# A hybrid attention encoder on one core: rotary's exchange moved from DMA to ScalarE, attention steps placed later, output casts ordered behind V's copy

## The chip, the cores and the metric

The kernel runs on one NeuronCore of one Trainium2 chip. The engines are named as in the profile: PE is TensorE's matrix multiply, PEld its weight load, DVE is VectorE, ACT is ScalarE, POOL is GpSimd, SP is SyncE, which issues this kernel's DMAs from one queue in order (SPq). Every engine takes its instructions in the order in which they stand in its program. The metric is the time of one execution on the device in microseconds.

## The reference

One encoder layer is applied to two groups of requests, a prompt of 1024 tokens and a sample of 256, each with 16 learned meta tokens in front. Cut to what matters:

```python
def encoder_layer(h, norm_w, w_in, q_norm_a, k_norm_a, q_norm_b, k_norm_b, rpb, w_out, rope_tabs):
    u = rms_norm(h, norm_w) @ w_in
    qa, ka, va, za, qb, kb, vb, zb = jnp.split(u, split_points(), axis=-1)
    qa = apply_axial_rope(rms_norm(qa.reshape(B, N, 8, 128), q_norm_a), rope_tabs)
    ka = apply_axial_rope(rms_norm(ka.reshape(B, N, 2, 128), k_norm_a), rope_tabs)
    ya = global_gqa(qa, ka, va) * jax.nn.silu(za)
    qb = rms_norm(qb.reshape(B, N, 8, 128), q_norm_b)
    kb = rms_norm(kb.reshape(B, N, 8, 128), k_norm_b)
    yb = neighbourhood_attention(qb, kb, vb, rpb) * jax.nn.silu(zb)
    return h + jnp.concatenate([ya, yb], axis=-1) @ w_out

def _rotate(x, cos, sin):
    x1, x2 = jnp.split(x, 2, axis=-1)
    return jnp.concatenate([x1 * c - x2 * s, x1 * s + x2 * c], axis=-1)
```

`h` has 2048 columns, a head has 128. The eight heads of group A (with two shared K/V heads) see all tokens; the eight of group B see a window of the grid and have a bias table `rpb`. Rotary works on each half of a head's 128 channels for itself: the first 32 channels of a half are combined with its last 32. With channels on the partitions, as here, the four blocks of 32 partitions are exchanged pairwise, 0 with 1 and 2 with 3.

## The kernel before, in words

**Arithmetic.** Everything is fp32. A product is made of three matmuls: each operand is cast by ACT to a high part (`split`, L65, L203) and DVE subtracts it from the original for a low part (L66); high x high, high x low and low x high are summed in PSUM (L219 to L221 in the projection, L368 to L370 and L409 to L411 in the attention, L1038 to L1040 in the output projection).

**Projection in strips.** `w_in` is cut into 52 strips of 128 columns: a head's K, Q, V or gate z of group A or B. Tokens form two chunks. Chunk one holds 512 (16 meta tokens, the sample, 240 of the prompt), chunk two the other 784, in blocks of 512 and 272. `strips` runs one strip: four weight chunks of 4 x 128 rows, each loaded by SP (L198), split into wh and wl, and used by 12 matmuls per block. In chunk one the low part is also stored (L210). After the second and the fourth weight chunk, that is twice a strip, it calls `run_due`, which starts what is due at that place: a head's scores, a head's values. Chunk two's attention of group B follows a list of such places too.

**Draining a strip.** `qk_evac` takes the strip's sum out of PSUM: ACT squares it into ms (L252), POOL sums over the partitions (L254, an all-reduce), DVE adds eps (L255), and `rsqrt` takes the inverse root (L72, L74, L75 on ACT, L76 and L77 on DVE). With rotary ACT also copies the sum times the gain to t (L258); four DMAs issued by SP copy t to ts with the blocks of 32 partitions exchanged (L261); DVE multiplies t by cosines (L263, in place) and ts by signed sines (L264), adds them (L265), and multiplies by the inverse root (L268). Then q or k is split. Rotary happens for 2 K and 8 Q strips in each chunk, with one block a strip in chunk one and two in chunk two: 30 drains. A strip of V is multiplied by the token scale into vt (`v_rows`, L280), transposed by PE in pieces of 128 columns into the PSUM tile tp, of which there is one (L287, L531), copied out by ACT (`rows_out`, L533, L538) and stored.

**Attention of chunk one.** After a head's Q strip `later` files the two halves of its attention under two later places: the scores and the softmax up to the sum under the first number of `PARTS`, the values and the output under the second, both counted in calls of `run_due` from there. `PARTS` is 2, 6. In group A two strips (z, q) lie between heads, in group B four. The attention is `attend` for group A and `attend_sample` for group B. An attention takes the maximum over partitions on POOL (L319), subtracts it on DVE (L388), takes exponentials on ACT (L389), sums (L334, L337 on POOL), splits the exponentials to ph and pl, and multiplies with V into po; `put_y` inverts the sum (L344 to L347) and stores the head's output (L355). While chunk one projects group B, `w_sums` also loads pieces of `w_out` and takes differences of them on DVE (L587), which are stored for the output projection.

**Output projection.** It runs in seven products over half matrices. `w_load` (L1012) brings a 128 x 512 piece of `w_out` into the buffers that the projection's x has left, `w_operand` splits it to wm (L65, L66), `y_load` (L976) brings an output tile in two halves, `y_operand` splits these, and `products` multiplies. The first sixteen pieces and the first tile are prepared while the last strips (V and then z of head 7 in group B) are still being projected. The last heads' attention runs beside the first product.

**Order.** The kernel is laid out by a scheduler at compile time, which runs a timing model of its own and orders each engine's instructions by it; `issue_after` and `add_manual_dep` with `NoSync` bind only the order on one engine.

Of the kernel before, what the change touches and what calls it, by code (L numbers as in the profile page):

```python
# [15 lines left out]
AF = mybir.ActivationFunctionType  # L16
ALU = mybir.AluOpType
# [27 lines left out]
WTYPE = (0, 1, 1, 2)  # L45
FILL = 1
LATE = 48
PARTS = 2, 6
WCH = 4
LAG = 6  # L50
TH = (NP + NS) // 2
# [1 line left out]
FB = 512  # L53
FH = DM // 2
QA, KA, VA, ZA, QB_, KB, VB, ZB = 0, 8, 10, 12, 20, 28, 36, 44
AGAIN = {KA, VA, ZA} | {a + h for a in (QB_, KB, VB, ZB) for h in range(4, 8)}


class Kern:
# [3 lines left out]
    def split(self, hi, lo, full):  # L63
        nc = self.nc
        self.hi = nc.scalar.copy(hi, full).ins  # L65
        return nc.vector.tensor_tensor(out=lo, in0=full, in1=hi.bitcast(F32), op=ALU.subtract).ins  # L66

    def rsqrt(self, ms, n):

        nc = self.nc  # L70
        l = self.ev.tile([P, n], F32, tag="ev", name="rs_l")
        nc.scalar.activation(l[:], ms, AF.Ln)  # L72
        r0 = self.ev.tile([P, n], F32, tag="ev", name="rs_r0")
        nc.scalar.activation(r0[:], l[:], AF.Exp, scale=-0.5)  # L74
        nc.scalar.activation(l[:], r0[:], AF.Square, scale=0.5 ** 0.5)  # L75
        nc.vector.tensor_tensor(out=l[:], in0=ms, in1=l[:], op=ALU.mult)  # L76
        nc.vector.scalar_tensor_tensor(out=r0[:], in0=l[:], scalar=1.5, in1=r0[:], op0=ALU.subtract, op1=ALU.mult)  # L77
        return r0
# [105 lines left out]
    def strips(self, jobs, getx):  # L184
# [4 lines left out]
        for c in range(KT // WCH):  # L189
            ws = []  # L190
            behind = self.behind.pop(0) if self.behind else None
            for j, (s, _, _) in enumerate(jobs):
                wp = self.w if j < 2 else self.w1
                with tc.high_priority(offset=self.woff), tc.issue_after(behind) if behind else nullcontext():
# [5 lines left out]
                    wl = wp.tile([P, WCH, P], F32R, tag="wl", name="wl")  # L200
                    if self.second and s not in AGAIN:
                        nc.sync.dma_start(wl[:].bitcast(F32), self.wld[s][:, c * WCH:(c + 1) * WCH, :])
# [5 lines left out]
                ws.append((wh, wl))  # L208
                if not self.second and s not in AGAIN:
                    nc.sync.dma_start(self.wld[s][:, c * WCH:(c + 1) * WCH, :], wl[:].bitcast(F32))  # L210
# [38 lines left out]
    def qk_evac(self, ps, o, n, wc, rope, segs, full=None):  # L249
        nc = self.nc  # L250
        ms = self.ev.tile([P, n], F32, tag="ev", name="ms")
        nc.scalar.activation(ms[:], ps[:, :n], AF.Square, scale=P ** -0.5)  # L252
        m2 = self.ev.tile([P, n], F32, tag="ev", name="m2")
        nc.gpsimd.partition_all_reduce(m2[:], ms[:], P, RED.add)  # L254
        nc.vector.tensor_tensor(out=m2[:], in0=m2[:], in1=self.eb[:, o:o + n], op=ALU.add)  # L255
        if rope is not None:
            t = self.ev.tile([P, n], F32, tag="ev", name="t")
            nc.scalar.activation(t[:], ps[:, :n], AF.Copy, scale=wc)  # L258
            ts = self.ev.tile([P, n], F32, tag="ev", name="ts")
            for i in range(4):  # L260
                nc.sync.dma_start(ts[32 * i:32 * i + 32], t[32 * (i ^ 1):32 * (i ^ 1) + 32])  # L261
            c, s = rope
            nc.vector.tensor_tensor(out=t[:], in0=t[:], in1=c, op=ALU.mult)  # L263
            nc.vector.tensor_tensor(out=ts[:], in0=ts[:], in1=s, op=ALU.mult)  # L264
            nc.vector.tensor_tensor(out=t[:], in0=t[:], in1=ts[:], op=ALU.add)  # L265
        r = self.rsqrt(m2[:], n)
        if rope is not None:
            nc.vector.tensor_tensor(out=r[:], in0=t[:], in1=r[:], op=ALU.mult)  # L268
        else:
            d = r[:] if full is None else full  # L270
            nc.vector.scalar_tensor_tensor(out=d, in0=ps[:, :n], scalar=wc, in1=r[:], op0=ALU.mult, op1=ALU.mult)
        for a, m, hi, lo in segs:
            if lo is None:
                nc.sync.dma_start(hi, r[:, a:a + m])
            else:
                self.split(hi, lo, r[:, a:a + m])

    def v_rows(self, ps, o, n):
        vt = self.ev.tile([P, n], F32, tag="ev", name="vt")
        self.nc.vector.tensor_tensor(out=vt[:], in0=ps[:, :n], in1=self.rb[:, o:o + n], op=ALU.mult)  # L280
        return vt

    def v_turn(self, vt, offs, m=P):
# [237 lines left out]
    def rows_out(self, vt, n, dst, o):  # L521

        nc = self.nc
        for a in range(0, n, 4 * P):
            offs = range(a, min(n, a + 4 * P), P)
            full = [x for x in offs if x + P <= n]
            t = self.ev.tile([P, 4, P], F32, tag="ev", name="vl")
            tp = self.tp.tile([P, 4, P], F32, tag="tp", name="tp")
            for i, x in enumerate(offs):
                m = min(P, n - x)  # L530
                self.turn_ins(nc.tensor.transpose(tp[:m, i, :], vt[:, x:x + m], self.ident[:]).ins)  # L531
            f = len(full)
            nc.scalar.copy(t[:, :f, :], tp[:, :f, :])  # L533
            nc.sync.dma_start(dst[o + a:o + a + P * f].rearrange("(t p) d -> p t d", p=P), t[:, :f, :])
            if f < len(offs):
                m = n - offs[f]
                t = self.ev.tile([m, P], F32, tag="ev", name="vl")
                nc.scalar.copy(t[:], tp[:m, f, :])  # L538
                nc.sync.dma_start(dst[o + n - m:o + n], t[:])
# [67 lines left out]
    def chunk1(self):  # L607
        nc, io = self.nc, self.io
# [1 line left out]
        self.due, self.late, self.turn, self.behind, self.turned, self.tie = iter(()), [], False, [], [], (1, 0)  # L610
        self.woff, self.second, self.projected, self.sums = 0, False, 0, self.w_sums()
        self.scale2 = [self.one2.tile([P, T2], F32, tag=n, name=n) for n in ("rb2", "eb2")]
        self.xsq = {}
        self.start_chunk(T1)
        vm3s = self.vm3s
        self.vm3s = vm3s + [self.v.tile([P, P], F32R, tag="vmz", name="vm3")]
# [93 lines left out]
        def later(h, args):  # L710
            def parts():
                yield from run(h, *args())
            g = parts()
            for n in PARTS:
                self.put(n, next, g, None)
# [264 lines left out]
    def y_operand(self, p, t, r):  # L980
        nc = self.nc
        if p in (1, 2):
            his, los, full = [], r, [l[:].bitcast(F32) for l in r]
            for l, f in zip(los, full):
                his.append(self.w.tile([P, WCH, P], F32R, tag="wh", name="yh"))
                self.split(his[-1][:], l[:], f)
            return his, los
        if p == 4:
            v = r[0]
        elif p == 7:  # L990
            v = r[0]
            nc.vector.tensor_tensor(out=v, in0=v, in1=r[1], op=ALU.subtract)
        else:
            v = self.ysum[t][:]
            a, b, op = {5: (r[0], r[-1], ALU.add), 6: (v, r[0], ALU.subtract), 3: (r[0], v, ALU.subtract)}[p]
            nc.vector.tensor_tensor(out=v, in0=a, in1=b, op=op)
        his, los = [], []
        for i in range(2):
            his.append(self.w.tile([P, WCH, P], F32R, tag="wh", name="yh"))
            los.append(self.w.tile([P, WCH, P], F32R, tag="wl", name="yl"))  # L1000
            self.split(his[i][:], los[i][:], v[:, WCH * i:WCH * i + WCH])
        return his, los
# [11 lines left out]

    def w_operand(self, r):
        w = self.x.tile([P, 2, FB], F32R, tag="xa", name="wm", align_bytes=ALIGN)
        self.split(w[:, 0, :], w[:, 1, :], r)
        return w

    def x_load(self, p, t, b):  # L1020

        if p not in (2, 7, 3, 4):
            return None
        o = self.ob.tile([P, FB], F32, tag="o", name="o")
        c, h = {2: (0, 0), 7: (1, 1), 3: (1, 0), 4: (0, 1)}[p]
        self.nc.sync.dma_start(o[:], self.io["xr"][:, NT * h + t, FH * c + FB * b:][:, :FB])
        return o
# [286 lines left out]
```

## Time and profile before

| what | value |
|---|---|
| median of 3 runs | 2173.13 us (2171.66 to 2174.37) |
| the profiled execution | 2170.17 us |
| its span, first to last instruction | 2168.4 us |
| granted TensorE clock | 1.000 |
| busy PE / DVE / ACT / POOL | 2154.2 / 1644.9 / 1115.1 / 522.7 us |

The span is what the views of the trace show; the execution's own time is 1.8 us longer. Lines such as L261 are lines of the kernel. In a group or a timeline row, `t<-pp` means that t is written from pp; `[1.64 <-ACT ph L65]` means that the engine stood idle for 1.64 us before and that the instruction named ended that wait. `x120` is a count. Matmuls overlap, so one of 0.39 us can follow another after 0.23 us.

### The profile page before, as it was taken

What the parts mean: (1) busy time and instruction counts of PE and PEld (TensorE: products, weight loads), DVE (VectorE), ACT (ScalarE), POOL (GpSimd) and SP (SyncE); (2) the same over time, 40 slices, a digit from 0 to 9 for tenths busy, and PEclk for the clock granted to TensorE, in tenths of its full rate; (3) what the DMA queues carried; (4) which work ended last, traced back from release to release, by engine and by line L of the source; (5) the groups of instructions that cost most, each with busy time, mean ns of one, the idle gap of its engine ahead of it and who ended that gap; (6) DMA issues with size and microseconds to landing.
All of it is one profiled execution on the core that took longest, in us unless ns stands there. A gap on an engine that the chain in (4) does not pass through costs nothing.

```text
span 2168.4 us, 34088 instructions
## 1 busy us (share of the span) xinstructions
PE 2154.2 (99%) x11745; PEld 1877.5 (87%) x11745; DVE 1644.9 (76%) x2989; ACT 1115.1 (51%) x2291; POOL 522.7 (24%) x250
## 2 busy tenths in 40 slices
PE   9999999999999999999999999999999999999999
PEld 7888878888888999989999999999999988888887
DVE  7787886777874899896798998677787877545763
ACT  6565554555554666665666666444443454232230
POOL 1232331221311234332133324324333312000000
PEclk9999999999999999999999999999999999999999
DMA  8667789988664333334333344654443364662663
GB/s 301 220 206 224 235 301 308 325 286 278 214 195 144 100 115 107 113 114 132 106 110 106 105 124 145 192 162 131 132 133 122 115 201 152 238 226 99 233 223 107
DMA packets 263182, 383.83 MB, mean 177 GB/s; under 512 B 44992, under 2 KB 112992, under 8 KB 263008
## 3 DMA queue, kind: packets, MB, share of 16 engines
q1 hardware_dynamic: 263008, 381.65, 54.1%
q8 instruction: 92, 1.51, 0.3%
q14 instruction: 82, 0.67, 0.1%
HBM read 281.01 MB, written 100.38 MB: 176 GB/s over the span
## 4 chain that ended last, share of the span: by engine, by line
PE 92%; DVE 3%; DMA 2%; ACT 1%; POOL 1%; issue 1%; SPq 0%; DVEq 0%; POOLq 0%; ACTq 0%
PE pp L219 20%; PE pp L221 20%; PE pp L220 20%; PE pq L1038 6%; PE pq L1040 6%; PE pq L1039 6%; PE po L510 2%; PE sp L476 2%; PE po L409 1%; PE sp L369 1%; PE sp L368 1%; PE po L411 1%; PE po L410 1%; PE sp L370 1%; POOL tot L337 1%
## 5 line engine op out<-in xcount | busy, mean ns | idle before, releaser
L219 PE MATMUL pp<-x,wh 128*128 128x512 f32 (+1 forms) x1664 | 654.5, 395 | 1.7 <-ACT x L162 1.1
L221 PE MATMUL pp<-x,wl 128*128 128x512 f32 (+1 forms) x1664 | 647.9, 390 | 1.1 <-DVE wl L66 1.1
L220 PE MATMUL pp<-x,wh 128*128 128x512 f32 (+1 forms) x1664 | 647.8, 390 | 0.0
L221 PEld LDWEIGHTS pp<-x,wl 128*128 128x128 f32 x1664 | 312.7, 188 | 62.7 <-DVE wl L66 2.0
L219 PEld LDWEIGHTS pp<-x,wh 128*128 128x128 f32 x1664 | 312.5, 188 | 59.3 <-ACT wh L65 2.6
L220 PEld LDWEIGHTS pp<-x,wh 128*128 128x128 f32 x1664 | 313.0, 188 | 52.8
L254 POOL PARTITION_ALL_REDUCE m<-ms x78 | 231.6, 2969 | 406.9 <-ACT ms L252 329.5
L66 DVE TENSOR_TENSOR wl<-wr,wh 128x512 fp32r<-128x512 f32 (+2 forms) x287 | 216.8, 758 | 114.6 <-ACT wh L65 102.2
L337 POOL PARTITION_ALL_REDUCE tot<-a x80 | 182.8, 2285 | 463.3 <-DVE a L334 447.1
L65 ACT CAST wh<-wr 128x512 fp32r<-128x512 f32 (+2 forms) x287 | 174.1, 611 | 202.3 <-PE pp L220 182.3
L220 PE MATMUL pp<-xb,wh 128*128 128x272 f32 x832 | 240.3, 289 | 0.0
L221 PE MATMUL pp<-xb,wl 128*128 128x272 f32 x832 | 239.6, 288 | 0.0
L219 PE MATMUL pp<-xb,wh 128*128 128x272 f32 x832 | 239.5, 288 | 0.0
L1038 PE MATMUL pq<-wm,yh 128*128 128x512 f32 x560 | 218.3, 390 | 0.0
L1040 PE MATMUL pq<-wm,yl 128*128 128x512 f32 x560 | 218.2, 390 | 0.0
L1039 PE MATMUL pq<-wm,yh 128*128 128x512 f32 x560 | 218.0, 389 | 0.0
L319 POOL PARTITION_ALL_REDUCE ma<-m x80 | 101.0, 1262 | 382.1 <-DVE m L317 381.6
L219 PEld LDWEIGHTS pp<-xb,wh 128*128 128x128 f32 x832 | 156.5, 188 | 7.6
L220 PEld LDWEIGHTS pp<-xb,wh 128*128 128x128 f32 x832 | 156.5, 188 | 7.4
L221 PEld LDWEIGHTS pp<-xb,wl 128*128 128x128 f32 x832 | 157.4, 189 | 0.3
L1040 PEld LDWEIGHTS pq<-wm,yl 128*128 128x128 f32 x560 | 105.1, 188 | 21.8
L1039 PEld LDWEIGHTS pq<-wm,yh 128*128 128x128 f32 x560 | 105.1, 188 | 21.7
(211 smaller groups left out, 3840.1 us busy)
## 6 DMA issues: line engine op xcount, KB each, us to landing
wr<-in_w_in SPq DMA_DIRECT2D x413, 256.0 KB, 3.4
wld<-wl SPq DMA_DIRECT2D x132, 256.0 KB, 4.2
wl<-wld SPq DMA_DIRECT2D x132, 256.0 KB, 3.1
yr<-yd SPq DMA_DIRECT2D x35, 512.0 KB, 4.8
wq<-in_w_out SPq DMA_DIRECT2D x64, 256.0 KB, 5.3
td<-wq SPq DMA_DIRECT2D x64, 256.0 KB, 4.5
ww<-td SPq DMA_DIRECT2D x64, 256.0 KB, 5.3
ww<-in_w_out SPq DMA_DIRECT2D x48, 256.0 KB, 5.2
```

Source lines behind the costliest of these rows:

```text
L65: self.hi = nc.scalar.copy(hi, full).ins
L66: return nc.vector.tensor_tensor(out=lo, in0=full, in1=hi.bitcast(F32), op=ALU.subtract).ins
L219: nc.tensor.matmul(p[:, :n], wh[:, k, :], xh[:, :n], start=first, stop=False)
L220: nc.tensor.matmul(p[:, :n], wh[:, k, :], xl[:, :n], start=False, stop=False)
L221: self.lastmm = nc.tensor.matmul(p[:, :n], wl[:, k, :], xh[:, :n], start=False, stop=last).ins
L254: nc.gpsimd.partition_all_reduce(m2[:], ms[:], P, RED.add)
L319: nc.gpsimd.partition_all_reduce(ma[:], m1[:], P, RED.max)
L337: nc.gpsimd.partition_all_reduce(tot[:], a1[:], P, RED.add)
L476: nc.tensor.matmul(dst, k[:, o:o + P], qfv[:, a:e, :], start=True, stop=True)
L1038: nc.tensor.matmul(ps, yh, wh, start=k == 0, stop=False)
L1039: nc.tensor.matmul(ps, yh, wl, start=False, stop=False)
L1040: self.lastmm = nc.tensor.matmul(ps, yl, wh, start=False, stop=k == 7).ins
```

## The change

Three edits. `PARTS` becomes 3, 7. In `qk_evac` the four DMAs from t to ts are replaced by four ACT passes that read 32 partitions of the PSUM sum each and write them, times their gain, to the exchanged place of ts. And two kinds of splits are ordered: those of `w_operand` number 5 to 16, and those of `y_operand` for the first tile of the first product. Their ACT casts go behind the copies of the last V strip on ACT: behind the next to last of the large copies while at most eight pieces are made, behind the last one after that. Their DVE subtractions go behind the last product vt of that strip.

```diff
-PARTS = 2, 6
+PARTS = 3, 7
...
+WFIRST = 5
...
+    def place_after(self, i, j, why):
+        self.tc.add_manual_dep(i, j.name, mybir.DependencyInfo(
+            mybir.DependencyClass.NoSync, mybir.DependencyReason.DATA), reason=why)
...
             for i in range(4):
-                nc.sync.dma_start(ts[32 * i:32 * i + 32], t[32 * (i ^ 1):32 * (i ^ 1) + 32])
+                j = 32 * (i ^ 1)
+                nc.scalar.activation(ts[32 * i:32 * i + 32], ps[j:j + 32, :n], AF.Copy, scale=wc[j:j + 32])
...
-        self.nc.vector.tensor_tensor(out=vt[:], in0=ps[:, :n], in1=self.rb[:, o:o + n], op=ALU.mult)
+        self.lastvt = self.nc.vector.tensor_tensor(out=vt[:], in0=ps[:, :n], in1=self.rb[:, o:o + n], op=ALU.mult).ins
...
-            nc.scalar.copy(t[:, :f, :], tp[:, :f, :])
+            self.vlcopies.append(nc.scalar.copy(t[:, :f, :], tp[:, :f, :]).ins)
...
-                self.split(his[-1][:], l[:], f)
+                i = self.split(his[-1][:], l[:], f)
+                if (p, t) == (1, 0):
+                    self.behind_v(i)
...
-        self.split(w[:, 0, :], w[:, 1, :], r)
+        i = self.split(w[:, 0, :], w[:, 1, :], r)
+        self.wouts += 1
+        if WFIRST <= self.wouts <= 16:
+            self.behind_v(i)
         return w
+
+    def behind_v(self, i):
+        self.place_after(i, self.lastvt, "drain first")
+        self.place_after(self.hi, self.vlcopies[-1 if self.wouts > 8 else -2], "drain first")
```

More of the change, by code (lines that the diff above doesn't have):

```diff
@@ L612, in chunk1 @@
         self.scale2 = [self.one2.tile([P, T2], F32, tag=n, name=n) for n in ("rb2", "eb2")]
-        self.xsq = {}
+        self.xsq, self.vlcopies, self.wouts = {}, [], 0
         self.start_chunk(T1)
```

## The prediction

> **What bounds the kernel now.** I read the page first: shares, then the chain that ended last.
>
> ```profile
> span 2168.4 us, 34088 instructions
> ...
> PE 2154.2 (99%) x11745; PEld 1877.5 (87%) x11745; DVE 1644.9 (76%) x2989; ACT 1115.1 (51%) x2291; POOL 522.7 (24%) x250
> ...
> PE 92%; DVE 3%; DMA 2%; ACT 1%; POOL 1%; issue 1%; SPq 0%; DVEq 0%; POOLq 0%; ACTq 0%
> ```
>
> TensorE is the bound. All its idle time is 2168.4 - 2154.2 = 14.2 us, and the change removes no matmul, so it can win only from those 14.2. Who makes PE wait is in the view of waits, PE alone (total, times, longest):
>
> ```profile
> PE po L409 <- ACT ph L65: 2.6, 3, 1.6
> PE tp L531 <- DVE vt L280: 2.3, 1, 2.3
> ...
> PE pp L221 <- DVE wl L66: 1.1, 2, 0.6
> PE tp L287 <- DVE vt L280: 1.1, 1, 1.1
> ...
> PE sp L368 <- DVE mx L376: 0.3, 1, 0.3
> ```
>
> These five make 2.6 + 2.3 + 1.1 + 1.1 + 0.3 = 7.4 us and are all that the three edits can touch; the rest lies at the start and where chunk two begins. The windows of 50 us (sum of window, then busy PE, PEld, DVE, ACT, POOL) say where:
>
> ```profile
> 250.00:300.00 50.00, 45.38 (x208) 35.67 (x207) 43.47 (x77) 24.68 (x55) 17.88 (x7) 1.00 0.82 271
> 300.00:350.00 50.00, 50.00 (x229) 41.47 (x228) 36.01 (x60) 22.31 (x44) 12.50 (x5) 1.00 0.92 308
> ...
> 1150.00:1200.00 50.00, 50.00 (x329) 45.96 (x328) 43.41 (x80) 31.17 (x64) 21.42 (x10) 1.00 0.34 105
> ...
> 1750.00:1800.00 50.00, 47.68 (x260) 41.62 (x259) 36.91 (x76) 27.49 (x56) 8.44 (x5) 1.00 0.64 207
> ```
>
> Two windows hold nearly all of it: 250 to 300 loses 50 - 45.38 = 4.62 us, 1750 to 1800 loses 2.32. The PE timeline names the first:
>
> ```profile
> 254.42 0.39 PE L409 MATMUL po<-ph,vs 128*128 128x256 f32 x1 [1.64 <-ACT ph L65]
> ...
> 260.44 0.28 PE L368 MATMUL sp<-qs,kc 128*128 128x256 f32 x1
> ...
> 282.38 0.39 PE L409 MATMUL po<-ph,vs 128*128 128x256 f32 x1 [0.77 <-ACT ph L65]
> ```
>
> With the two waits at L221 and the one at L287, which lie between them, that is 1.64 + 1.1 + 1.1 + 0.77 = 4.61, so the 4.62 is one cascade. Its head is the wait for head 6's exponentials. Followed back on the timelines of ACT, SP, POOL and DVE:
>
> ```profile
> 243.27 0.67 ACT L258 ACTIVATE t<-pp,nqkw 128x496 f32<-128x496 f32 x1
> ...
> 248.44 1.26 SPq L261 DMA_DIRECT2D ts<-t  x2
> ...
> 243.46 3.76 POOL L254 PARTITION_ALL_REDUCE m<-ms  x1 [5.04 <-ACT ms L252]
> 247.69 2.21 POOL L319 PARTITION_ALL_REDUCE ma<-m  x1 [0.47 <-POOL m L254]
> ...
> 251.61 0.67 DVE L263 TENSOR_TENSOR t<-t,rope 128x496 f32<-128x496 f32 x1 [2.64 <-DMA ts<-t]
> 252.21 0.68 DVE L388 TENSOR_TENSOR S<-S,ma 128x512 f32<-128x512 f32 x1
> ...
> 253.77 0.60 ACT L65 CAST ph<-S 128x512 fp32r<-128x512 f32 x1
> ```
>
> Rotary's copy t of head 7 is ready at 243.27 + 0.67 = 243.94. Its last two exchange DMAs issue only at 248.44, behind other transfers on SP, and the product at L263, which overwrites what they read, stands at the head of DVE for 2.64 us. Behind it stands L388 of head 6, whose maximum was ready at 247.69 + 2.21 = 249.90. So the DMA, not the softmax, made L388 2.3 us late (252.21 - 249.90), more than the 1.64 that PE then waits. What is late next is the head's sum, hence its output:
>
> ```profile
> 264.04 2.21 DVE L346 TENSOR_TENSOR tot<-tot,r 128x256 f32<-128x256 f32 x1 [2.67 <-ACT r L345]
> ...
> 260.97 0.39 SPq L198 DMA_DIRECT2D wr<-in_w_in  x1
> ...
> 267.19 0.37 SPq L355 DMA_DIRECT2D yd<-y  x1
> 267.79 0.33 SPq L198 DMA_DIRECT2D wr<-in_w_in  x1
> ```
>
> SP holds weight loads behind the store at L355, so none issues from 260.97 to 267.79; that starves wl (L221), and the DVE queue then delays vt and the next ph.
>
> **The change part by part.**
>
> *Rotary without DMA.* Removed and added pieces by their rows (tile view of ts, groups by form):
>
> ```profile
> L261 SPq DMA_DIRECT2D ts<-t x120: 507/582/627, 45.1 to 1260.9; - x120
>   DVE t L263: 11.6, 8
> ...
> L258 ACT ACTIVATE t<-pp,nqkw 128x512 f32<-128x512 f32 x12 | 8.2, 685 | 0.0
> L258 ACT ACTIVATE t<-pp,nqkw 128x496 f32<-128x496 f32 x8 | 5.4, 670 | 0.0
> L258 ACT ACTIVATE t<-pp,nqkw 128x272 f32<-128x272 f32 x10 | 4.8, 482 | 0.0
> ...
> L254 POOL PARTITION_ALL_REDUCE m<-ms x78 | 231.6, 2969 | 406.9 <-ACT ms L252 329.5 <-DMA wl<-wld 41.3 <-DMA wld<-wl 12.5
> ```
>
> SP loses 120 issues of 0.582 = 70 us, DVE loses up to 11.6 us of waiting. ACT gains four passes for each of the 30 of L258. No row shows a pass over 32 lanes; its cost lies between nothing and a full L258, and I take the full one, since the instruction streams the same columns: 4 x (12 x 0.685 + 8 x 0.670 + 10 x 0.482) = 73.6 us, ACT from 51% to 55%. On the path they cost nothing as long as POOL covers them: the all-reduce of the same drain takes 2.97 us in the mean and 3.76 here, the four passes 2.7 at most, and the logarithm behind them waits for the all-reduce anyhow. With that cover gone a drain is late by 2.7 and whatever ACT has queued behind it too, weight casts among them; bounds on PE 0 and +2.7 us (one drain of the thirty uncovered), value 0. The bank of the drained block is held 2.7 us longer; pp has four, and a chunk-one strip uses one, so the next user comes three strips later. From 243.94 the exchange would end near 246.6 (four passes of 0.670) rather than 251.6, so L388 follows the maximum directly.
>
> *PARTS 3, 7.* No instruction is added. Scores and values come half a strip later: 24 matmuls of 0.23 (the step at 1773.27 below), 5.5 us. Their interval by the list is unchanged. But values of head 6 and scores of head 7 stand at the same place of it, the former start at 254.42 and the latter at 260.44: the scores run 6 us late, when rotary has delivered q. Moved by 5.5 they start about on time, so the softmax gains as much room before its values. Both edits serve the same cascade; either alone would about cover the 1.64 at its head. Together: bounds -4.6 and 0 (the loss beyond is a rival), value -4.4, near the full end, because the rows tie each later wait to the first; 0.2 is left for the extra load on DVE (43.47 of 50), which does not go away. For what is left of L409 (2.6 - 1.64 - 0.77 = 0.2) and L368's 0.3, in chunk two: bounds -0.5 and +1 (twice as much in new ones), value -0.4, as DVE there loses the same DMA waits.
>
> *w_out's casts behind V's copy.* At the end of the projection:
>
> ```profile
> 1768.12 0.58 ACT L533 COPY vl<-tp 128x512 f32<-128x512 f32 x1
> ...
> 1768.86 0.43 DVE L280 TENSOR_TENSOR vt<-pp,rb 128x272 f32<-128x272 f32 x1
> ...
> 1767.54 0.50 SPq L976 DMA_DIRECT2D yl<-yd  x1
> ...
> 1773.57 0.62 ACT L65 CAST yh<-yl 128x512 fp32r<-128x512 f32 x1 [0.84 <-DMA yl<-yd]
> ...
> 1773.27 0.39 PE L1038 MATMUL pq<-wm,yh 128*128 128x512 f32 x1
> 1773.50 0.39 PE L1039 MATMUL pq<-wm,yh 128*128 128x512 f32 x1
> ```
>
> V's copy and its last product stand behind w_out casts that themselves wait for loads, and the transposes wait 2.32 us for both. Put first, they cost DVE 0.43 and ACT 0.58 at a moment when the casts wait for DMA anyway, and the 2.32 goes. What is late next is y's second half: its cast ends at 1774.19, its low part near 1774.9 (0.68 more, what L388 takes for the same size). The fifth product needs it 12 matmuls of 0.23 = 2.8 us after the first, now 1776.0; with PE 2.3 earlier at 1773.7. V's stores now stand ahead of it on SP, two or three issues of some 0.4 (0.37 for L355). So 0.9 comes back: -1.4, bounds -2.3 and +1.
>
> **Sum**: -4.4 - 0.4 - 1.4 + 0 = -6.2 us, a span of 2162.2. The profiled execution took 2170.17, 1.8 over its span; the median of the runs is 2173.13, 3 above. The same difference on the median: 2166.9.
>
> **Rivals.** *One: the cascade only moves.* Heads 6 and 7 now meet w_out's differences (L587) half a strip deeper, where DVE is 43.47 of 50 busy. Against it: the 2.64 at its head is gone. Then -0.4 - 1.4 = -1.8: 2171.3.
>
> *Two, slower: strip ends collide.* With 3 and 7 odd, scores and values of all chunk-one heads fall at the end of a strip, with that strip's drain, which now also carries ACT's four passes; so far they came in mid-strip. If the casts' lead over PE runs out there, a cascade like this one (4.62) starts. For it: one such lead did run out, after 267.79. Against it: 50.00 of 50 from 300 on, with ACT at 22.31. It decides from two new cascades on, with the old one kept: +9.2 - 1.8 = +7.4: 2180.5.
>
> *Three: rotary's products meet the all-reduce.*
>
> ```profile
> 244.47 2.06 DVE L301 TENSOR_TENSOR zs<-z,za 128x256 f32<-128x256 f32 x1
> ...
> L301 DVE TENSOR_TENSOR zs<-z,za 128x256 f32<-128x256 f32 x16 | 8.4, 526 | 1.5 <-ACT za L299 1.0
> ```
>
> An L301 of 0.526 took 2.06 inside the all-reduce of 243.46. L263 came after it (251.61) and would now come near 246.6, inside: 1.5 us more on DVE for each of 30 drains, 46 us. DVE at 43.41 in chunk two has 6.6 us of 50 left, so most is hidden; two waits of 1.5 there and one in chunk one: -6.2 + 4.6 = -1.6: 2171.5. [...]
>
> **How the numbers follow.** The forecast gets 0.57, the moved cascade 0.14, the all-reduce 0.06, the collision 0.23. About 0.2%, 4.3 us, can be told from no change: faster 0.57, same 0.20, slower 0.23. The forecast's own range: all 7.4 won and the runs' spread of 1.5 below, 2164.2; half won, 2170. The low end is put at 2162, since the 14.2 - 7.4 = 6.8 us of PE's other idle time may give a third too. The high end, 2177, takes in rivals one and three and a collision with a single cascade.
>
> **What would show it.** Right: the window 250 to 300 near 50 for PE, no DVE wait at L263 on DMA, no issues at the old L261, ACT near 1189 us, and no L531 wait on vt; a short PE wait at L1038 or L1040 on y. Wrong: waits at L409 or L221 that return elsewhere in chunk one (rival two or one), or L263 far over its 0.67 (rival three).

## The result, and the profile after

The changed kernel takes 2165.9 us (median of 5 runs, 2163.48 to 2166.97), the kernel before 2173.13 (5 runs, 2171.66 to 2175.73): 0.9967 of its time, 95% interval 0.9956 to 0.9979, or 7.2 us less. The forecast was 2166.9. The profiled execution of after is its slowest, 2166.97 with a span of 2165.2, and that of before (2170.17) lay below all its five runs, so the two traces lie only 3.2 us apart. Line numbers moved: L263 is now L269, L409 is L415, L531 is L537, L533 and L538 are L539 and L544, L1038 is L1053.

The page of after: span, busy time by engine, the chain that ended last.

```profile
span 2165.2 us, 33975 instructions
...
PE 2154.3 (99%) x11745; PEld 1879.6 (87%) x11745; DVE 1657.4 (77%) x2989; ACT 1187.4 (55%) x2411; POOL 519.3 (24%) x250
...
PE 98%; DMA 1%; DVE 1%; SPq 0%; ACT 0%; issue 0%; DVEq 0%; ACTq 0%
```

The waits of PE in after (total, times, longest):

```profile
PE pq L1053 <- ACT vl L544: 3.8, 1, 3.8
PE warm L630 <- DVE wz L627: 1.2, 1, 1.2
PE pp L224 <- ACT x L167: 1.1, 1, 1.1
PE pp L224 <- ACT wh L66: 0.7, 3, 0.4
PE tp L293 <- DVE vt L286: 0.3, 1, 0.3
```

The five waits of the cascade have shrunk to one of 0.3, chunk two's are no longer listed, the wait for vt at the end is gone. At the top stands one that before did not have: 3.8 us for V's last copy. The two windows in which before lost its time say the same (window, sum, busy PE, PEld, DVE, ACT, POOL with counts, PEclk, DMA share, GB/s):

```profile
250.00:300.00 50.00, 49.71 (x236) 41.41 (x235) 40.21 (x70) 24.10 (x52) 19.27 (x8) 1.00 0.78 257
1750.00:1800.00 50.00, 46.23 (x230) 39.33 (x229) 34.40 (x70) 26.55 (x53) 6.70 (x5) 0.93 0.63 203
```

PE is idle for 0.29 us in the first, where it was for 4.62, and for 3.77 in the second, where it was for 2.32, with a granted clock of 0.93 on top. The first gained more than its idle time: 236 matmuls instead of 208 are 28 more, 6.4 us at the 0.227 of a steady step (23 steps from 1773.27 to 1778.48 in before; the mix of sizes is not quite the same, so this is an estimate).

**Why the cascade is gone.** Timelines of after around the head that was late before (start, duration, engine, line; the wait before it in brackets):

```profile
234.15 0.67 ACT L263 ACTIVATE t<-pp,nqkw 128x496 f32<-128x496 f32 x1
234.34 3.63 POOL L259 PARTITION_ALL_REDUCE m<-ms  x1 [6.69 <-ACT ms L257]
234.84 2.70 ACT L267 ACTIVATE ts<-pp,nqkw 32x496 f32<-32x496 f32 x4
235.22 2.31 DVE L269 TENSOR_TENSOR t<-t,rope 128x496 f32<-128x496 f32 x1
...
246.45 0.68 DVE L394 TENSOR_TENSOR S<-S,ma 128x512 f32<-128x512 f32 x1
...
249.14 0.61 ACT L66 CAST ph<-S 128x512 fp32r<-128x512 f32 x1
...
256.28 0.28 PE L415 MATMUL po<-ph,vs 128*128 128x256 f32 x1
```

The four passes end at 237.54, inside the all-reduce that ends at 237.97. Before, t of this block stood at 243.27, its exchange ended only at 251.61, and DVE stood on it. The drain itself now starts 9.1 us sooner too: ACT squares the strip (L257) at 233.67, soon after PE has finished it, where before it did the casts of head 6's q, a gate and a copy of scores first. Now the exponentials of head 6 are split at 249.14, and the values that need them start at 256.28 without a wait. The product at L269 does what rival three expected: it lies inside the all-reduce and takes 2.31 us instead of 0.67.

**What went wrong at the end.** The same views of after where the output projection begins:

```profile
1756.83 0.43 DVE L286 TENSOR_TENSOR vt<-pp,rb 128x272 f32<-128x272 f32 x1
...
1758.87 0.49 PE L537 MATMUL tp<-ident,vt 128*128 128x128 f32 x3
...
1760.30 0.81 SPq L982 DMA_DIRECT2D yl<-yd  x1
...
1766.13 0.62 ACT L66 CAST yh<-yl 128x512 fp32r<-128x512 f32 x1 [3.15 <-DMA yl<-yd]
1766.65 0.37 ACT L539 COPY vl<-tp 128x256 f32<-128x256 f32 x1
...
1766.92 0.25 ACT L544 COPY vl<-tp 16x128 f32<-16x128 f32 x1
...
1767.22 0.80 PE L1053 MATMUL pq<-wm,yh 128*128 128x512 f32 x1 [3.77 <-ACT vl L544]
```

V's product is early and its transposes run at 1758.87, as forecast. But the last two copies of tp stand on ACT behind the cast of y's second half, which waits 3.15 us for its load, and the first output product needs tp, of which there is one. The edit put y's casts behind the next to last large copy only; the copy that PE waits for comes after them. Then the clock, in windows of 4 us of after:

```profile
1766.00:1770.00 4.00, 2.78 (x7) 2.21 (x8) 3.22 (x6) 3.87 (x10) 0.00 (x0) 0.52 1.03 363
1770.00:1774.00 4.00, 4.00 (x13) 3.15 (x12) 4.00 (x8) 3.65 (x9) 0.00 (x0) 0.62 0.57 164
1774.00:1778.00 4.00, 4.00 (x24) 3.50 (x23) 2.39 (x7) 2.27 (x5) 0.00 (x0) 1.00 0.54 162
```

After the stall the granted clock is 0.52 and 0.62, and products of 128x512 start 0.43 us apart (1769.52, 1769.95), where at a clock of 1.00 it is 0.23 (1774.13, 1774.36). The stall costs more than its 3.77: the first output product starts 6.05 us sooner than before (1767.22, then 1773.27), but the span ends only 3.2 sooner. The other 2.8 were lost behind the stall, where no wait of PE is listed.

**What the passes cost.** The rows of the line view (durations: least, median, most; first and last start; forms) for the pass over 32 lanes and the copy over 128:

```profile
L267 ACT ACTIVATE ts<-pp,nqkw x120: 477/667/686, 45.0 to 1247.5; 32x512 f32<-32x512 f32 x48, 32x272 f32<-32x272 f32 x40, 32x496 f32<-32x496 f32 x32
...
L263 ACT ACTIVATE t<-pp,nqkw x30: 479/672/692, 44.3 to 1245.5; 128x512 f32<-128x512 f32 x12, 128x272 f32<-128x272 f32 x10, 128x496 f32<-128x496 f32 x8
```

A quarter of the lanes cost the same here (0.667 and 0.672 us in the median), as the forecast took it. ACT is up 72.3 us for 73.6 forecast.

### The profile page after: what moved, and what is told of

The parts are those of the page before. It is cut to its first block, busy times and chain, and to the rows that moved or that the text cites. A ratio compares the mean times of both kernels' runs of the same rounds, so it can differ in the third digit from the quotient of the medians.

```text
span 2165.2 us, 33975 instructions
## 1 busy us (share of the span) xinstructions
PE 2154.3 (99%) x11745; PEld 1879.6 (87%) x11745; DVE 1657.4 (77%) x2989; ACT 1187.4 (55%) x2411; POOL 519.3 (24%) x250
## 4 chain that ended last, share of the span: by engine, by line
PE 98%; DMA 1%; DVE 1%; SPq 0%; ACT 0%; issue 0%; DVEq 0%; ACTq 0%
PE pp L224 22%; PE pp L226 22%; PE pp L225 22%; PE pq L1053 6%; PE pq L1055 6%; PE pq L1054 6%; PE po L516 2%; PE sp L482 2%; PE sp L375 1%; PE sp L376 1%; PE sp L374 1%; PE po L417 1%; PE po L416 1%; PE po L415 1%; DMA wr<-in_w_in 0%; PE tp L537 0%
## 5 line engine op out<-in xcount | busy, mean ns | idle before, releaser
L259 POOL PARTITION_ALL_REDUCE m<-ms x78 | 223.1, 2860 | 363.7 <-ACT ms L257 306.4
L1053 PE MATMUL pq<-wm,yh 128*128 128x512 f32 x560 | 219.7, 392 | 3.8 <-ACT vl L544 3.8
L325 POOL PARTITION_ALL_REDUCE ma<-m x80 | 111.2, 1390 | 451.4 <-DVE m L323 442.7
L1053 PEld LDWEIGHTS pq<-wm,yh 128*128 128x128 f32 x560 | 105.8, 189 | 25.9 <-ACT vl L544 4.2
L1054 PEld LDWEIGHTS pq<-wm,yh 128*128 128x128 f32 x560 | 105.9, 189 | 22.0
```

The costliest lines, as they stand in the source:

```text
L325: nc.gpsimd.partition_all_reduce(ma[:], m1[:], P, RED.max)
L1053: nc.tensor.matmul(ps, yh, wh, start=k == 0, stop=False)
L1054: nc.tensor.matmul(ps, yh, wl, start=False, stop=False)
```

## The experiments

The kernel before was timed beside each. Its medians were 2171.73 (with the first four below), 2171.96 (one number of `PARTS`, and the DMA by ScalarE), 2171.86 (doubled passes, and y's second half behind V) and 2172.24 (the last two).

**Rotary by ScalarE alone.** The four ACT passes, `PARTS` and the casts as before.

> Rotary's exchange by ScalarE alone, PARTS 2, 6 and the cast order of before. Theory (the exchange DMA that blocks DVE is the head of the cascade at 250 to 283 us): PE is busy at least 49 of 50 us in the window 250 to 300 (before 45.38, after 49.71), the waits of 0.2 and 0.3 in chunk two go as well, and the tail keeps its wait of 2.3 us on vt; the time is 4 to 6 us under before. Rival (the later places of PARTS cured the cascade): the window stays near 46 and the time within 2 us of before.

Measured: 2169.17 (2168.1 to 2170.7), ratio 0.999 (0.9981 to 1.0); PE is busy for 46.16 of 50 us in 250 to 300. So rotary without DMA wins some 2.6 of the 7 us, by an interval that just reaches no change, and the window is far from the 49 that was expected. Timelines of this kernel:

```profile
248.85 3.87 POOL L338 PARTITION_ALL_REDUCE tot<-a  x1 [6.07 <-DVE a L335]
...
252.75 0.42 ACT L345 ACTIVATE r<-tot 128x256 f32<-128x256 f32 x1 [3.69 <-POOL tot L338]
...
254.03 0.40 ACT L65 CAST qs<-rs_r 128x256 fp32r<-128x256 f32 x1
...
254.48 0.39 PE L369 MATMUL sp<-qs,kc 128*128 128x256 f32 x1 [1.41 <-ACT qs L65]
...
278.97 0.28 PE L288 MATMUL tp<-ident,vt 128*16 128x128 f32 x1 [2.43 <-DVE vt L281]
```

With q early the scheduler puts head 7's scores right behind head 6's values. But q's split stands on ACT behind the inverse of head 6's sum (L345), which waits 3.69 us for POOL. The wait has changed its name; chunk two's waits are gone, though.

**PARTS alone.**

```diff
-PARTS = 2, 6
+PARTS = 3, 7
```

> PARTS 3, 7 alone, exchange by DMA and the cast order of before. Theory: DVE still waits for the exchange DMA, but the softmax has half a strip more room, so about half of the cascade goes: PE busy 47 to 49 in the window 250 to 300, time 1 to 4 us under before. Rival (PARTS is the cure): window near 50, 4 to 6 us under before. Rival (strip ends collide): new waits in chunk one, time at or over before.

Measured: 2173.55 (2171.93 to 2174.52), ratio 1.0006 (0.9996 to 1.0015): nothing. The row of the tile view of ts in this kernel that names who waited for the exchange:

```profile
  DVE t L263: 15.5, 13
```

The DMA is waited for no less than before (11.6, 8 then), and 250 to 300 stays at 46.05.

**The casts alone.** Only `behind_v` and its calls.

> The order of w_out's and y's casts alone; exchange by DMA, PARTS 2, 6. Theory (V's last copies stand behind y's second cast on ScalarE and hold the PSUM tile that the first output product writes): the wait on vt goes, a PE wait of 3 to 4 us on the last copy vl takes its place, with the granted clock at 0.5 for some microseconds behind it; time 2 to 5 us over before. Rival (the tail's new wait comes from the new timing of the projection): no such wait, time 1 to 2.5 us under before.

Measured: 2173.36 (2170.68 to 2174.5), ratio 1.0004 (0.9995 to 1.0013). First row of its PE waits:

```profile
PE pq L1052 <- ACT vl L543: 3.3, 1, 3.3
```

The wait for vt (2.3) is gone and this one stands in its place: it comes from the order of the casts itself and needs none of the other edits.

**Rotary and PARTS, without the casts.**

> After without the order of the casts: rotary by ScalarE and PARTS 3, 7. Theory: chunk one as in after (49.7 of 50 at 250 to 300), the tail as in before (2.3 us on vt), so the best of these four: 2 to 5 us under after, near 2162. Rival (the order of the casts is worth its 2.3 us): 1 to 2 us over after, near 2168.

Measured: 2164.81 (2162.52 to 2165.17), ratio 0.9965 (0.9952 to 0.9977). All that the change wins is here, and it needs both edits: -2.6 and +1.8 alone, -6.9 together. After's median is 1.1 us higher than this one, but so was its kernel before, by 1.4 (2173.13 against 2171.73); each against its own, after wins 7.2 and this one 6.9. So the casts add nothing that can be told, either way.

**Which of the two numbers of PARTS.** Rotary by ScalarE, casts as before, with 3, 6 (scores later alone) and with 2, 7 (values later alone).

> Rotary by ScalarE with the cast order of before and PARTS 3, 6: the scores half a strip later, values where they were. With the exchange by ScalarE and PARTS 2, 6 the scores of head 7 waited 1.4 us for q; with 3, 7 nothing waited. Theory (the scores' place is what has to move, since the list now places them ahead of q): the wait on qs goes, but the softmax has half a strip less, so values wait for ph in chunk one: PE busy 47 to 49 at 250 to 300, time 2 to 4 us over rotary with 3, 7. Rival (only the scores matter): 49.7 there and the time of rotary with 3, 7 within 1.5 us.

> Rotary by ScalarE with the cast order of before and PARTS 2, 7: values half a strip later, scores where they were. Theory: the wait of the scores on qs stays, and what head 6's output delays (q's split behind the inverse of the sum on ScalarE) now comes later, so the wait on vt behind it shrinks: PE busy 47 to 49 at 250 to 300, 2 to 4 us over rotary with 3, 7. Rival (values are what had to move): 49.7 and the time of rotary with 3, 7 within 1.5 us.

Measured: 3, 6 gives 2167.91 (2166.2 to 2170.98), 0.9981 (0.9971 to 0.999); 2, 7 gives 2163.65 (2162.56 to 2165.9), 0.9961 (0.9946 to 0.9975). The window of each, scores first:

```profile
250.00:300.00 50.00, 47.39 (x211) 39.09 (x210) 40.48 (x70) 23.82 (x51) 17.68 (x7) 0.93 0.79 257
```

```profile
250.00:300.00 50.00, 50.00 (x238) 41.86 (x237) 40.73 (x74) 25.52 (x53) 18.26 (x7) 1.00 0.82 266
```

With the scores alone moved, values come half a strip closer to their scores, and PE waits for them; a row of that kernel's PE timeline:

```profile
276.19 0.39 PE L412 MATMUL po<-pl,vs 128*128 128x256 f32 x1 [1.27 <-DVE pl L66]
```

With the values alone moved there is no wait left in this window. Room ahead of the values is what was short, not room ahead of the scores.

**The exchange by DMA, issued by ScalarE instead of SP**, with `PARTS` 3, 7.

```diff
-                nc.sync.dma_start(ts[32 * i:32 * i + 32], t[32 * (i ^ 1):32 * (i ^ 1) + 32])
+                nc.scalar.dma_start(ts[32 * i:32 * i + 32], t[32 * (i ^ 1):32 * (i ^ 1) + 32])
```

> The exchange by DMA as before, but issued by ScalarE instead of SP, with PARTS 3, 7 and the cast order of before. It tells the queue from the transfer. Theory (SP's backlog is what makes the exchange late; the issues came 1.2 to 5.2 us after t, the transfer itself takes 2): DVE's wait shrinks to some 2 us less what lies between, the window 250 to 300 is near 49.5, time within 3 us of rotary by ScalarE passes with 3, 7. Rival (any DMA in this place is too late): waits on qs and vt as with PARTS 3, 7 alone, time at before.

Measured: 2175.15 (2173.47 to 2176.01), ratio 1.0012 (1.0003 to 1.0022). Who waited for ts, and the time from issue to landing:

```profile
  ACT wh L65: 9.5, 5
  DVE t L263: 8.0, 9
...
DMA to landing us min/median/max: 1.8/2.7/6.1
```

DVE waits about half as long as with `PARTS` alone (8.0 for 15.5). But past SP's queue the DMA lands after 2.7 us in the median and 6.1 at most (2.0 and 4.2 before), now weight casts on ACT wait for it too, and PE waits 4.4 us for a k behind that. So SP's queue alone was not the trouble. The queue of a third engine was not tried; that any transfer in this place is too late is therefore not shown.

**Each ACT pass twice.**

```diff
-                nc.scalar.activation(ts[32 * i:32 * i + 32], ps[j:j + 32, :n], AF.Copy, scale=wc[j:j + 32])
+                for _ in range(2):
+                    nc.scalar.activation(ts[32 * i:32 * i + 32], ps[j:j + 32, :n], AF.Copy, scale=wc[j:j + 32])
```

> After, with each of rotary's four passes done twice: 120 ScalarE instructions more, some 73 us of ScalarE. Theory (the passes lie beside the all-reduce and cost PE nothing): the first four are hidden, eight take 5.4 us a drain against an all-reduce of 3, so the drains are late by 2 to 2.7 us and PE shows at most a wait or two near 250 us: within 2 us of after. Rival (ScalarE's queue is the next bound, the passes delay weight casts): waits of PE on wh or wl in chunk one, 5 us or more over after.

Measured: 2180.27 (2180.19 to 2180.79), ratio 1.004 (1.0026 to 1.0053), 14.4 us over after (15.6 when each is taken against its own kernel before), where 2 at most were expected. First PE waits:

```profile
PE pq L1054 <- ACT vl L545: 3.8, 1, 3.8
PE pp L224 <- DVE kcf L278: 2.1, 1, 2.1
PE po L418 <- DVE pl L67: 2.0, 3, 1.2
PE po L416 <- ACT ph L66: 1.5, 3, 0.7
PE pp L224 <- DVE rs_r L278: 1.5, 2, 0.8
```

Four passes hide behind the all-reduce (2.70 us and 3.63 in the drain above), eight (some 5.4 us, from 0.667 each) don't: k and q come late in chunk one, and in chunk two the exponentials too. The cover is about as wide as the passes, and ACT's 55% does not show that. How much of it is the drain itself, and how much ACT's queue with 73 us more in it, this run does not separate.

**y's second half behind V too.** After, with `behind_v` taking a flag that sends y's second cast behind the last copy, which now includes the partial one.

```diff
-                nc.scalar.copy(t[:], tp[:m, f, :])
+                self.vlcopies[-1] = nc.scalar.copy(t[:], tp[:m, f, :]).ins
...
-                    self.behind_v(i)
+                    self.behind_v(i, len(his) == 2)
...
-        self.place_after(self.hi, self.vlcopies[-1 if self.wouts > 8 else -2], "drain first")
+        self.place_after(self.hi, self.vlcopies[-1 if last or self.wouts > 8 else -2], "drain first")
```

> After, with the cast of y's second half also behind the last of V's copies. Theory (the first product waits for the PSUM tile that V's copies free): the wait on vl goes; the copies take place near 1760, the first product starts some 3.5 us earlier and waits 0.5 to 1.5 us inside for y's second half; the clock is not cut; 4 to 7 us under after, near 2160. Rival (the product's start waits for the output operands themselves): PE waits as long as in after, now on yh or yl, and the time is that of after within 1.5 us.

**The same, and the second eight w_out pieces loaded behind y.**

```diff
         load_y(0)
+        first = self.lasty
         for j in range(16):
...
-            load_w(0, j)
+            with self.tc.issue_after(first) if j >= 8 else nullcontext():
+                load_w(0, j)
```

> As e5, with the loads of w_out's pieces 9 to 16 issued behind the load of y's second half. If y's second half is what is late next in e5, its wait goes and the time is 0.5 to 1.5 us under e5; if pieces 9 to 16 are just as tight, the wait moves to wm in the second product and the time is that of e5 within 1 us.

Measured: 2162.42 (2161.6 to 2162.55), ratio 0.9956 (0.9943 to 0.9968), and 2160.56 (2160.04 to 2161.28), ratio 0.9948 (0.9935 to 0.9962). The last window of the first:

```profile
1750.00:1800.00 50.00, 50.00 (x263) 42.81 (x262) 38.19 (x80) 29.44 (x61) 7.91 (x6) 1.00 0.71 227
```

No wait and no cut of the clock: 263 matmuls instead of 230. So V's last copy was the whole loss at the end. What the loads' order adds (1.9 us between the medians, with no run in common) does not show in the two profiled spans, 2159.5 and 2159.2; where it comes from stays open.

**The best of it with the scores at their old place** (`PARTS` 2, 7 in the kernel just above).

> The kernel that loads w_out's second half behind y (2160.56) with chunk one's scores back at their old place and the values half a strip later alone. Theory: with rotary by ScalarE the values' place is what keeps 250 to 300 us busy (50.00 with the values moved alone, 49.71 with both moved), so moving the scores buys nothing: 2159.0 to 2161.0, PE 49.9 or more of 50 in 250 to 300 us, no wait of PE over 1 us inside. Rival: the scores' old place, one exchange earlier, meets the q split now and then: window 49 or less and 2162 or more.

Measured: 2160.28 (2160.13 to 2161.36), ratio 0.9945 (0.9932 to 0.9959), no wait of PE over 1 us but one at the start and one where chunk two begins. The scores' move is worth nothing that can be measured. This and the one above beat both kernels.

**The end alone.** The kernel before with the casts of the best version and nothing else.

> The kernel before (rotary's exchange by DMA, scores and values at their old places) with w_out's casts and both of y's casts behind V's last copy, and w_out's second half loaded behind y. Theory: the three stretches add up, so the order of the casts, with y's second half put behind V too, is worth here what it was beside the new rotary (from 2164.81 to 2160.56, 4.2 us): 2167.0 to 2168.5, no wait of PE between 1750 and 1800 us over 1 us, and 45 to 46 of 50 us in 250 to 300 as before. Rival: the gain at the end was the clock's more than the wait's, and the kernel before, whose clock was not cut at the end, has less to win: 2169.5 or more.

Measured: 2168.4 (2166.85 to 2170.42), ratio 0.9983 (0.9974 to 0.9992). Its two windows:

```profile
250.00:300.00 50.00, 46.14 (x212) 36.30 (x211) 44.26 (x79) 24.83 (x55) 17.89 (x7) 1.00 0.81 271
1750.00:1800.00 50.00, 50.00 (x274) 43.80 (x273) 37.26 (x80) 27.79 (x55) 8.52 (x5) 1.00 0.67 217
```

The end, done right, is worth 3.8 us by itself, the cascade and chunk two 6.9: together 10.7, and the best version wins 11.3 of its kernel before. The parts add up.

## Why the prediction was right, and where it was not

**Rotary without DMA and PARTS: right, and too small.** The chain of cause (late exchange, L388 held, softmax, output, weights) was right: these waits went with the DMA, though with rotary alone others came in their place. -4.8 was said for the cascade and chunk two, -6.9 was measured. The sum counted PE's idle time alone, 4.62, and 0.4 for chunk two. The two traces tell more. A transposition of V in the strip behind the cascade starts at 327.26 before and at 321.30 after, 5.96 sooner; the first of the last V strip at 1761.48 and 1754.02, 7.46 sooner. So the cascade gave some 6 us and what lies between, chunk two above all, some 1.5. What exceeds the 4.33 of idle time that went (4.62 less 0.29) are steps that were stretched by more than their idle gap. A matmul counts as busy for 0.38 or 0.39, where the next followed after 0.22 or 0.23: in before the starts at 252.41 and 254.42 lie 2.01 apart, of which 1.64 counts as idle, and those at 270.94 and 271.26 lie 0.32 apart with no idle time between them (the first counts as busy for 0.48).

**"Either alone would about cover the 1.64 at its head": wrong.** One edit alone gives -2.6, the other nothing. With rotary alone a split waits behind a sum on ACT (1.41) and another cascade follows (2.43); with PARTS alone DVE still stands on the DMA (15.5). The sum was not touched by it, since it took both together. Nor was the argument about the scores what decided: the values' move carries the gain.

**The passes at 0: right in value, the cover narrower than it reads.** A 32-lane pass cost what a full one cost (0.667 and 0.672 us) and was hidden. The bound of +2.7 for lost cover, one drain of thirty, was far too small: with the passes doubled, and the cover of every drain gone, the price was 14.4.

**w_out's casts behind V's copy, -1.4: the step that failed.** The wait for vt went, as said. y's second half was late, as said, its cast ending at 1766.75. But the step asked only when the fifth product would need that half (0.9 back). It did not ask what stands behind that cast on ACT: V's last copies, which free the bank of the first product. So 3.8 came back for the 2.3 won, and the lower clock with it (0.93 in the window of 50 us, where before had 1.00). Alone the edit measured +1.6 on the medians, which its interval does not tell from nothing; on top of the others it is +1.1 by the medians and -0.3 with each against its own kernel before. The gain of 1.4 did not come. The result is right by size because this and the surplus of the cascade and chunk two (2.1) nearly cancel, and that is luck.

**Rivals.** That the cascade only moves holds for rotary alone, not for the pair. The collision at strip ends did not come: the list of waits has no new one but that at L1053. What rival three expected is there without its price. By form, before and after, the product with the cosines (busy, mean ns, idle before it):

```profile
L263 DVE TENSOR_TENSOR t<-t,rope 128x512 f32<-128x512 f32 x12 | 8.8, 736 | 5.9 <-DMA ts<-t 3.4 <-issue 2.3
...
L263 DVE TENSOR_TENSOR t<-t,rope 128x496 f32<-128x496 f32 x8 | 5.4, 672 | 8.3 <-DMA ts<-t 8.2
```

```profile
L269 DVE TENSOR_TENSOR t<-t,rope 128x512 f32<-128x512 f32 x12 | 12.9, 1076 | 10.7 <-ACT t L263 10.7
L269 DVE TENSOR_TENSOR t<-t,rope 128x496 f32<-128x496 f32 x8 | 12.1, 1514 | 0.5 <-ACT t L263 0.5
```

The two forms grow by 10.8 us, and DVE by 12.5 in all, against the 46 that the rival assumed; no PE wait comes of it.

## What to carry to other kernels

When an instruction is placed ahead of others by hand, list what stands behind it on its engine up to the last one that somebody waits for: an order that lets the first copies go ahead but leaves the last one behind a load won nothing here. A cascade's gain can exceed the idle time that the waits name, so compare the number of matmuls in the window as well, or the start of the same instruction in both traces. And a cover is measured by doubling what it hides, not by the share at which the engine is busy.

## What the runs showed of the hardware that was not expected

After some short stalls of PE the granted clock was lower for a few microseconds, after others it was not. The longest PE wait in the window and the mean granted clock there, over 50 us, from the profiles of before, of after and of the experiments:

| kernel, window | PE wait, us | PEclk |
|---|---|---|
| before, 1750 to 1800 | 2.3 | 1.00 |
| rotary alone, 250 to 300 | 2.4 | 0.97 |
| rotary alone, 1750 to 1800 | 2.5 | 0.97 |
| scores later, 250 to 300 | 1.3, and 1.3 right behind | 0.93 |
| scores later, 1750 to 1800 | 2.8 | 0.97 |
| DMA by ScalarE, 250 to 300 | 4.4 | 0.97 |
| rotary and PARTS, 1750 to 1800 | 2.6 | 0.97 |
| PARTS alone, 1750 to 1800 | 2.9 | 1.00 |
| values later, 1750 to 1800 | 3.1 | 0.93 |
| casts alone, 1750 to 1800 | 3.3 | 0.93 |
| after, 1750 to 1800 | 3.8 | 0.93 |

In after the lower clock lasted from 1766 to 1773: in windows of 1 us it is 0.59 in the first of these and 0.50 in each of the other six. By the windows of 4 us shown above it fell short of 1.00 by 4 x 0.48 + 4 x 0.38 = 3.4 us of full clock. With rotary and PARTS two windows of 5 us, from 1760 to 1770, have 0.83 each: 2 x 5 x 0.17 = 1.7 us. From these two, the loss of matmul time on top of the wait is estimated at some 1.7 us where the table has 0.97 and 3.4 where it has 0.93.

The longest wait does not order these rows. Rotary alone had 2.4 us and a clock of 0.97, `PARTS` alone 2.9 and 1.00; with the scores later, two waits of 1.3 went with 0.93, as did 3.8 in after. So whether a stall of 2 to 3 us cost more than itself differed from run to run here. What decided it, and why the loss was 1.7 us in some and 3.4 in others, the runs do not show.

The VectorE product in the all-reduce of 234.34 (2.31 us instead of 0.67) ends at 237.53, 0.44 us before the all-reduce does by the profile (237.97). So it was slowed, but not held to the end. Ends on POOL are rough in a profile, so this is a sign and not a proof.
